# Two transformer blocks on one core: 128-row score products in block 2, and the order inside groups of small products

## The chip, the cores and the metric

The kernel runs on 1 core of a Trainium2 chip. The metric is device time in microseconds from launch to end, taken as the median of several runs. TensorE does the matrix products, VectorE and ScalarE the element-wise work, GpSimd a few powers and some transfers, and the DMA queues bring the weights. A profile of one execution goes with the times.

## The reference

The input is 256 rows of 1024 numbers. It passes through two layers of a first block (bidirectional mLSTM and dilated attention, a gated output, then a SwiGLU), and after them through two layers of a second block, which the change mostly concerns. A layer of the second block is

```
h = rms_norm(x); z, xbc, dt, q, k, v = split(h @ w_in)
xs, B, C = silu(conv7(xbc))                 # 16 heads of 64, 2 groups of 128 states
y_ssm  = ssd(xs, dt, B, C) forward + backward + d * xs;  y_ssm = rms_norm(y_ssm * silu(z))
s      = q k^T / 8 + bias(distance), |i-j| <= 128       # 16 heads of 64, 4 key heads
y_attn = softmax(s with a sink logit) @ v
x = x + [y_ssm, y_attn] @ w_out
h = rms_norm(x); x = x + (silu(conv3(h @ w_g)) * (h @ w_u)) @ w_down
```

Everything is in fp32. Activations and weights of the large products are split into a high part in fp32r (the rounded value) and a low part (the rest), and a product is three matmuls: high by high, low by high, high by low.

## The kernel before, in words

One core does all of it in one pass. Weights arrive in chunks of 1 MB in the order of `make_plan`; `emit_load` splits each half of a chunk, ScalarE making `hi` and VectorE `lo` (L473). `lin_st` (L520 to L522) multiplies a chunk with the normalized input and leaves pairs of 128 x 256 results in a PSUM bank (`lst`); `lin_units` (L612 to L614) does the output projections (`wo`, `ffo`). These are TensorE's bulk.

The order on each engine is made at build time. The framework lists instructions by priority and by when their inputs should be ready; `prio` raises or lowers the priority of a named kind of work, with the numbers of `PRIO1` and `PRIO2`. So small products are put between the large ones wherever the list finds them ready, and at run time each engine goes through its list in order, standing still where an input is missing.

A layer of block 2 runs in `mixer2` and `ffn2`. `mixer2` goes through the projections in the order of `PUMPS` and between them takes pieces of work from two lists:

- SSD, `ssd_quarter`: `mats` makes the decay matrices of a head (`sM`), `prod` (L1573) multiplies them with the inputs `xd` of two heads, one head in output partitions 0 to 63, one in 64 to 127, into the bank `sy`. A group is 8 products in plain fp32, each of which is two records in the trace.
- Attention, `attn`: `score(i)` makes the scores of one head for two blocks of 128 queries. The query tile `q2t` holds a head's 64 columns of q as fp32r in its own 64 partitions and the rest of the rounding in the other 64. The key tile `kst` holds the rounded key in both halves, so L1652 adds q_high k_high and q_low k_high in one product of 128 rows. L1653 adds q_high k_low from `kl`, which stands in the head's own 64 partitions only: a product with 64 rows. A group is L1652, L1653, L1652, L1653. `trans(i)` turns the probabilities (`qtr`, L1669: four transposes for two query blocks and two key blocks), `pv2_` (L1705) multiplies them with the values (`qo`: 8 products, two heads in the two halves of the output partitions), `rows_` spreads the softmax sums (`qrt`).

`keys` (L1777 to L1779) fills `kst` and `kl` once for each layer. Temporary tiles come from rings by size: `SHARED2` says how many buffers of each there are in block 2. The constants pool holds, among others, `cst` (identity, two triangles, and the mask of block 1's mLSTM in columns from `C_MK`) and the parameter vectors `pv1` of block 1; it lasts through the whole kernel. The temporary pool of block 1 is closed ahead of block 2's.

In block 1 the dilated attention's scores (`as`, L1221 and L1222) have 128 rows in both products, its values (`ao`, L1260) are 12 products with 64 output partitions, and the mLSTM's transposes are `mpt` (L1075).

Of the kernel before, what the change touches and what calls it, by code (L numbers as in the profile page):

```python
# [10 lines left out]
F32 = mybir.dt.float32  # L11
# [5 lines left out]
P = 128  # L17
T = 256
# [27 lines left out]
TR2 = (6, 4, 4)  # L46

SHARED1 = {512: 3, 1024: 5, 2048: 11, 4096: 5}
SHARED2 = {512: 3, 1024: 4, 2048: 11, 3072: 5, 4096: 2}

C_ID, C_TU, C_TL, C_MK = 0, 128, 256, 384
N_CST = 384 + 512

SEC = {"sh1": 0, "sc1": 1, "g1": 2, "sh2": 3, "sc2": 4, "g2": 5}

# [249 lines left out]
def two_blocks_kernel(ctx: ExitStack, tc: tile.TileContext, a: dict, out: bass.AP, stop=None):  # L305
# [5 lines left out]
    wp = ctx.enter_context(tc.tile_pool(name="weights", bufs=2))  # L311
    bp = ctx.enter_context(tc.tile_pool(name="big", bufs=8))
    pools = ExitStack()
    cur = {"tp": pools.enter_context(tc.tile_pool(name="tmp1", bufs=2)), "shared": SHARED1}
    lin = ctx.enter_context(tc.tile_pool(name="lin", bufs=4, space=bass.MemoryType.PSUM))
    sm = ctx.enter_context(tc.tile_pool(name="sm", bufs=4, space=bass.MemoryType.PSUM))
# [28 lines left out]
    ident = cst[:, C_ID:C_ID + P]  # L345
    triU = cst[:, C_TU:C_TU + P]
    triL = cst[:, C_TL:C_TL + P]
    mk = cst[:, C_MK:C_MK + 512]
    ones = cp.tile([P, P], F32, name="ones")
    V.memset(ones, 1.0)  # L350
    mhalf = cp.tile([P, 8], F32, name="mhalf")
# [8 lines left out]
    pv2 = []  # L360
    rw2 = []
    for l in range(DEPTH):
        pv1.append(cp.tile([P, a["pv1"].shape[2]], F32, name=f"pv1_{l}"))
        pv2.append(cp.tile([P, a["pv2"].shape[2]], F32, name=f"pv2_{l}"))
        rw2.append(cp.tile([P, 80], F32, name=f"rw2_{l}"))
    S.dma_start(pv1[0], a["pv1"][0])

    def late_params():
        S.dma_start(cst[:, P:], a["cst"][:, P:])
        S.dma_start(pv1[1], a["pv1"][1])  # L370
        for l in range(DEPTH):
            S.dma_start(pv2[l], a["pv2"][l])
            S.dma_start(rw2[l], a["rows2"][l:l + 1, :].to_broadcast([P, 80]))
# [575 lines left out]
    def mixer1(l, u, ob0=None, small=None, begun=None):  # L949
# [78 lines left out]
        def head(h, qT, kT, v):  # L1028
# [41 lines left out]

            def trans():
                tr = bank("mpt")
                for tt in range(2):
                    for c in range(2):
                        PE.transpose(tr[:, c * T + tt * P:c * T + (tt + 1) * P], s["p"][:, tt, c * P:(c + 1) * P],  # L1075
                                     ident)
                pt = tmp([2, T], "mPT")
                S.activation(pt, tr.rearrange("p (c t) -> p c t", c=2), AF.Copy)
                s["pt"] = pt
# [123 lines left out]
        def slots(j, qk):  # L1203


            s = {}
            sums = tmp([4], "asum")
            nm = tmp([4], "anm")
            r = tmp([4], "ar")

            def score(tt):
                def run():
                    tk = slice(tt * P, (tt + 1) * P)
                    sps = [bank("as") for _ in range(2)]
                    bs = []
                    for i in range(2):
                        bs.append(tmp([512], "abias"))
                        nc.sync.dma_start(bs[i], a["bt"][2 * j + i][:, tt, :])
                    for i in range(2):
                        q0, kh, kl = (qk[0][:, n, i, :] for n in range(3))  # L1220
                        PE.matmul(sps[i][:, :T], q0[:, tk], kh, start=True, stop=False)  # L1221
                        PE.matmul(sps[i][:, :T], q0[:, tk], kl, start=False, stop=True)  # L1222
                    for g in (1, 2):
                        for i in range(2):
                            o = sps[i][:, P + g * P:2 * P + g * P]
                            PE.matmul(o, qk[g][:, i, tk], qk["k"][:, g - 1, tk], start=True, stop=True)
                    for i in range(2):
                        e = 2 * tt + i
                        sp, b_ = sps[i], bs[i]
                        pt = tmp([512], "aP", bufs=4)  # L1230
                        V.tensor_tensor_reduce(pt, sp, b_, -1.0, -2 * NEG, ALU.add, ALU.min,
                                               nm[:, e:e + 1])
                        S.activation(pt, pt, AF.Exp, scale=-1.0, bias=nm[:, e:e + 1], accum_out=sums[:, e:e + 1])
                        s[i, tt] = pt
                return run

            def trans():
                V.reciprocal(r, sums)
                for i in range(2):
                    for b in range(2):  # L1240
                        tr = bank("apt")
                        for k in range(2):
                            for tt in range(2):
                                PE.transpose(tr[:, k * T + tt * P:k * T + (tt + 1) * P],
                                             s[i, tt][:, (2 * b + k) * P:(2 * b + k + 1) * P], ident)
                        pt = tmp([2, T], "aPT", bufs=4)
                        src = tr.rearrange("p (k t) -> p k t", k=2)
                        if b:
                            S.activation(pt, src, AF.Copy)
                        else:  # L1250
                            V.tensor_copy(pt, src)
                        s["t", i, b] = pt

            def pv_():
                o = bank("ao")
                for k, g, t0, n, vk in ((0, 0, 0, T, 0), (1, 0, 0, T, 1), (0, 1, 0, P, 0), (0, 1, P, P, 1),
                                        (1, 2, 0, P, 0), (1, 2, P, P, 1)):
                    for i in range(2):
                        c0 = (2 * j + i) * 64
                        PE.matmul(o[64 * i:64 * i + 64, t0:t0 + n], va[g][:, vk, c0:c0 + 64],  # L1260
                                  s["t", i, g > 0][:, k, t0:t0 + n], start=(k, g) == (0, 0), stop=(g, t0) == (2, P))
                for tt in range(2):
                    for i in range(2):
                        e = 2 * tt + i
                        PE.matmul(o[64 * i:64 * i + 64, T + tt * P:T + (tt + 1) * P],
                                  r[:, e:e + 1].to_broadcast([P, 64]), ident, start=True, stop=True)
                rb = tmp([T], "arb")
                S.activation(rb, o[:, T:], AF.Copy)
                os_ = tmp([T], "aos")
                V.tensor_tensor(os_, o[:, :T], rb, ALU.mult)  # L1270
                src = os_.rearrange("p (r i) -> p r i", r=2)
                dh = yb[0][:, j, :].rearrange("p (i r) -> p r i", r=2)
                dl = yb[1][:, j, :].rearrange("p (i r) -> p r i", r=2)
                S.activation(dh, src, AF.Copy)
                V.tensor_tensor(dl, src, dh.bitcast(F32), ALU.subtract)

            for n_, what, fn in zip(SLOT_AT, ("score", "score", "trans", "pv"), (score(0), score(1), trans, pv_)):
                defer(n_, with_prio("a_" + what, fn))
# [161 lines left out]
    def mixer2(l, u, zouts, small):  # L1440
# [95 lines left out]
        def ssd_quarter(i, xt):  # L1536
# [26 lines left out]
            def prod(pr):  # L1563
                def run():
# [3 lines left out]
                    xd = xds[i // 2][:, i % 2]  # L1568
                    o = s["y"][:, pr * T:(pr + 1) * T]
                    for d, c, m0, l0, n in ((0, 0, 0, 0, T), (1, 1, P, 0, T), (0, 1, T, P, P), (1, 0, 0, 0, P)):  # L1570
                        for k in range(2):
                            h = 2 * pr + k
                            PE.matmul(o[64 * k:64 * k + 64, l0:l0 + n], xd[:, d, c, 64 * h:64 * h + 64],  # L1573
                                      s[4 * i + h][:, d, m0:m0 + n], start=(d, c) == (0, 0), stop=(d, c) == (1, 0))
# [42 lines left out]
                made.update((c, c + 1))  # L1617

        kst = [tmp([2, T], f"kst{p}", F32R) for p in range(2)]
        kl = tmp([2, T], "kl", F32R)  # L1620
        vv = tmp([2, 256], "m_k")
        qts = {}

        def attn(c):
# [17 lines left out]
            def score(i):  # L1642
                def run():
                    hd = 4 * c + i
                    p = i % 2
                    own = slice(64 * p, 64 * p + 64)
                    kt = c // 2
                    sp = bank("qs")
                    pt = tmp([2, T], "qP", bufs=4)
                    for tt in range(2):  # L1650
                        q = qt[p][:, i // 2, tt * P:(tt + 1) * P]
                        PE.matmul(sp[:, tt * T:(tt + 1) * T], q, kst[p][:, kt, :], start=True, stop=False)  # L1652
                        PE.matmul(sp[:, tt * T:(tt + 1) * T], q[own], kl[own, kt, :], start=False, stop=True)  # L1653
                    for tt in range(2):
                        e = 2 * i + tt
                        w0 = 128 - 128 * tt
# [7 lines left out]
            def trans(i):  # L1664
                def run():
                    tr = bank("qtr")
                    for tt in range(2):
                        for k in range(2):
                            PE.transpose(tr[:, k * T + tt * P:k * T + (tt + 1) * P], s[i][:, tt, k * P:(k + 1) * P],  # L1669
                                         ident)  # L1670
# [28 lines left out]
            def pv2_():  # L1699
                o = bank("qo")  # L1700
                for pr in range(2):
                    for k in range(2):
                        for i in range(2):
                            kv = 2 * (c // 2) + i
                            PE.matmul(o[64 * i:64 * i + 64, pr * T:(pr + 1) * T], vv[:, k, kv * 64:(kv + 1) * 64],  # L1705
                                      s["t", 2 * pr + i][:, k, :], start=k == 0, stop=k == 1)
# [65 lines left out]
        def keys():  # L1772
            ps = st("k2")
            for p in range(2):
# [1 line left out]
                src = ps[own].rearrange("p (c t) -> p c t", c=2)  # L1776
                S.activation(kst[p][own], src, AF.Copy)  # L1777
                S.activation(kst[p][other], src, AF.Copy)
                V.tensor_tensor(kl[own], src, kst[p][own].bitcast(F32), ALU.subtract)  # L1779

        def values():
            w = chunk("v2", l)
# [135 lines left out]
```

## Time and profile before

| | |
|---|---|
| median of 3 runs | 1934.13 us (1933.36 to 1936.22) |
| profiled execution | 1935.3 us, span 1933.5 us, mean granted clock 0.997 |
| TensorE (PE) | 1890.2 us busy, 13022 matmuls |
| VectorE (DVE) | 1465.9 us busy |
| ScalarE (ACT) | 1085.0 us busy |
| DMA | 388.09 MB, mean 201 GB/s |

A row of the timeline gives the start in us from the span's first instruction, the duration, engine, line, operation, the tiles written and read, the form (rows times columns of the array, then the moving operand) and how many records are merged in it. Matmuls overlap in the array: a duration holds the passage through it, so the pace is read from the distance between two starts. PEld is the load of a product's stationary operand.

### The profile page before, as it was taken

Reading aid. Unit: us, or ns where it says so; the run is one execution under the profiler, and the core shown is the slowest. Engines: PE = TensorE matmul, PEld = TensorE weight load, DVE = VectorE, ACT = ScalarE, POOL = GpSimd, SP = SyncE. Lnnn points to the kernel's source line nnn. Section 1 sums busy time; section 2 is a strip of 40 time slices with the busy share of each in tenths; the row PEclk is TensorE's granted clock in tenths of the full one; section 3 lists DMA queues with packets and bytes.
Section 4 is the critical chain, followed back from the end, with each engine's and each line's share of the span. In section 5 each row is a group of like instructions: output and inputs, shape, how many; then the busy total and the mean of one; then the engine's idle time right before and its main releaser. Section 6 shows DMA issues by size and latency. Waiting matters only on the chain.

```text
span 1933.5 us, 32684 instructions
## 1 busy us (share of the span) xinstructions
PE 1890.2 (98%) x13022; PEld 1710.4 (88%) x13022; DVE 1465.9 (76%) x2555; ACT 1085.0 (56%) x1881; POOL 87.5 (5%) x108
## 2 busy tenths in 40 slices
PE   6999999999999999999999999999999999999998
PEld 5889999899978899999899888778998898779996
DVE  8888877787767787868766578877876688768763
ACT  3556654454436566544544457876554577756552
POOL 0000000200010000000200001000000000000000
PEclk9999999999999999999999999999999999999999
DMA  8654777487745446767377636444555454345552
GB/s 313 253 185 161 265 248 275 154 292 287 272 153 196 175 169 222 249 255 261 137 272 281 230 111 181 132 128 174 196 192 183 171 184 152 107 169 188 192 179 86
DMA packets 64202, 388.09 MB, mean 201 GB/s; under 512 B 7611, under 2 KB 12395, under 8 KB 21554
## 3 DMA queue, kind: packets, MB, share of 16 engines
q1 hardware_dynamic: 58064, 364.93, 52.3%
q0 software_dynamic: 4832, 20.13, 3.5%
q8 instruction: 102, 1.67, 0.3%
q10 hardware_dynamic: 1154, 0.95, 0.2%
q14 instruction: 50, 0.41, 0.1%
HBM read 384.82 MB, written 5.36 MB: 202 GB/s over the span
## 4 chain that ended last, share of the span: by engine, by line
PE 88%; DVE 5%; ACT 3%; DMA 1%; issue 1%; POOL 0%; POOLq 0%; DVEq 0%; ACTq 0%
PE lst L520 17%; PE lst L521 17%; PE lst L522 17%; PE ffo L613 4%; PE ffo L612 4%; PE ffo L614 4%; PE wo L612 2%; PE wo L613 2%; PE wo L614 2%; PE sy L1573 2%; PE qs L1653 1%; PE qo L1705 1%; PE avl L553 1%; PE avl L554 1%; PE avl L555 1%
## 5 line engine op out<-in xcount | busy, mean ns | idle before, releaser
L473 ACT ACTIVATE hi<-raw 128x1024 fp32r<-128x1024 f32 x546 | 571.7, 1057 | 499.0 <-PE lst L521 302.0
L473 DVE TENSOR_TENSOR lo<-raw,hi 128x1024 fp32r<-128x1024 f32 x546 | 662.5, 1221 | 229.5 <-ACT hi L473 228.7
L520 PE MATMUL lst<-uh,hi 128*128 128x256 f32 x2592 | 743.9, 287 | 0.0
L522 PE MATMUL lst<-uh,lo 128*128 128x256 f32 x2592 | 737.8, 285 | 0.2
L521 PE MATMUL lst<-ul,hi 128*128 128x256 f32 x2592 | 737.9, 285 | 0.0
L520 PEld LDWEIGHTS lst<-uh,hi 128*128 128x128 f32 x2592 | 496.6, 192 | 5.1 <-issue 3.9
L522 PEld LDWEIGHTS lst<-uh,lo 128*128 128x128 f32 x2592 | 496.7, 192 | 4.5 <-issue 3.5
L521 PEld LDWEIGHTS lst<-ul,hi 128*128 128x128 f32 x2592 | 496.8, 192 | 3.3 <-issue 2.1
L412 DVE CUSTOM_DVE_ANT_0 raw<-raw,crow,pv 128x1024 f32<-128x1024 f32 x96 | 120.9, 1280 | 27.6 <-DMA raw<-in_ws_dram 27.5
L612 PE MATMUL ffo<-hi,ffh 128*128 128x512 f32 x352 | 137.3, 390 | 0.0
L613 PE MATMUL ffo<-lo,ffh 128*128 128x512 f32 x352 | 137.0, 389 | 0.0
L614 PE MATMUL ffo<-hi,ffl 128*128 128x512 f32 x352 | 137.0, 389 | 0.0
L942 DVE SCALAR_TENSOR_TENSOR cacc<-cin,pv,cacc 128x254 f32<-128x254 f32 (+2 forms) x272 | 111.6, 478 | 0.3 <-ACT cacc L935 0.2
L614 PEld LDWEIGHTS ffo<-hi,ffl 128*128 128x128 f32 x352 | 66.1, 188 | 13.7
L612 PEld LDWEIGHTS ffo<-hi,ffh 128*128 128x128 f32 x352 | 66.1, 188 | 13.5
L613 PEld LDWEIGHTS ffo<-lo,ffh 128*128 128x128 f32 x352 | 66.1, 188 | 13.5
L774 DVE TENSOR_TENSOR ul<-uf,uh 128x256 fp32r<-128x256 f32 (+1 forms) x35 | 26.4, 755 | 26.7 <-ACT uh L769 26.7
L1555 ACT ACTIVATE sM<-arow,ac 128x128 f32<-128x128 f32 x128 | 44.9, 389 | 0.0
L1402 ACT ACTIVATE rsq<-xres 128x512 f32<-128x512 f32 x20 | 12.5, 627 | 53.3 <-DVE xres L1865 21.6
L553 PE MATMUL mvh<-hi,uh 128*128 128x512 f32 x80 | 33.4, 418 | 8.1 <-ACT uh L865 8.1
L555 PE MATMUL ltt<-hib,ul 128*128 128x512 f32 x72 | 29.7, 413 | 7.7 <-DVE ul L774 5.5
L766 ACT ACTIVATE uf<-tr,ub,us 128x128 f32<-128x128 f32 x36 | 14.3, 451 | 39.9 <-PE tr L752 39.9
(381 smaller groups left out, 3004.4 us busy)
## 6 DMA issues: line engine op xcount, KB each, us to landing
raw<-in_ws_dram SPq DMA_DIRECT2D x329, 1024.0 KB, 4.9
abias<-in_bt_dram SPq DMA_DIRECT2D x32, 256.0 KB, 4.7
arow<-scra POOLq DMA_DIRECT2D x32, 256.0 KB, 5.4
wtab<-skew SPq DMA_DIRECT2D x16, 384.0 KB, 3.6
gb<-in_rows_dram POOLq DMA_DIRECT2D x8, 512.0 KB, 5.8
skew<-scrt POOLq DMA_DIRECT2D x4, 1024.0 KB, 11.9
raw<-in_ws_dram SPq DMA_DIRECT2D x6, 512.0 KB, 8.9
grow<-scrg POOLq DMA_DIRECT2D x2, 1024.0 KB, 6.3
```

The source lines that it names most:

```text
L412: V.tensor_tensor_reduce(src, src, crow, 1.0, pv1[l][:, 136 + sec * 8 + ct:137 + sec * 8 + ct], ALU.mult, ALU.add, ada[l, sec][:, ct:ct + 1])
L473: fn()
L520: PE.matmul(outp, sh, mh, start=first, stop=False)
L521: PE.matmul(outp, sh, ml, start=False, stop=False)
L522: PE.matmul(outp, sl, mh, start=False, stop=last)
L553: PE.matmul(outs[tt], sl[0], hi[:, i, :], start=kt == first, stop=False)
L555: PE.matmul(outs[tt], sl[1], hi[:, i, :], start=False, stop=kt == last)
L612: PE.matmul(o, sh, hi[:, i, :], start=kt == first, stop=False)
L613: PE.matmul(o, sh, lo[:, i, :], start=False, stop=False)
L614: PE.matmul(o, sl, hi[:, i, :], start=False, stop=kt == last)
L942: V.scalar_tensor_tensor(acc[:, c, lo:hi], src[:, lo + s:hi + s], cw[:, k0 + j:k0 + j + 1], acc[:, c, lo:hi], ALU.mult, ALU.add)
L1555: S.activation(m[:, d, 2 * tt * P:(2 * tt + 1) * P], rt[:, d, hh, tt * P:(tt + 1) * P], AF.Relu, scale=-1.0, bias=ac[:, tt, col])
```

## The change

- `keys` makes `klt`, one tile for each parity of head, with the low part of the keys in both halves of the partitions; L1653 multiplies the whole query tile with it, 128 rows. That adds q_low k_low, which was left out before.
- One more buffer of 2 KB in block 2. The mask `mk` and `pv1` move to a pool of their own, which is closed with the temporaries of block 1; `mk` gets a transfer of its own.
- In five groups of small products the loops run so that the first product reads the input that is made last.

```diff
-SHARED2 = {512: 3, 1024: 4, 2048: 11, 3072: 5, 4096: 2}
+SHARED2 = {512: 3, 1024: 4, 2048: 12, 3072: 5, 4096: 2}
-N_CST = 384 + 512
+N_CST = 384
...
+    cp1 = pools.enter_context(tc.tile_pool(name="const1", bufs=1))
...
-    mk = cst[:, C_MK:C_MK + 512]
+    mk = cp1.tile([P, 512], F32, name="mk")
...
-        pv1.append(cp.tile([P, a["pv1"].shape[2]], F32, name=f"pv1_{l}"))
+        pv1.append(cp1.tile([P, a["pv1"].shape[2]], F32, name=f"pv1_{l}"))
...
-        S.dma_start(cst[:, P:], a["cst"][:, P:])
+        S.dma_start(cst[:, P:], a["cst"][:, P:N_CST])
+        S.dma_start(mk, a["cst"][:, C_MK:C_MK + 512])
...   block 1: head.trans (mpt)
-                for tt in range(2):
+                for tt in (1, 0):
...   block 1: slots.pv_ (ao)
-                for k, g, t0, n, vk in ((0, 0, 0, T, 0), (1, 0, 0, T, 1), (0, 1, 0, P, 0), (0, 1, P, P, 1),
-                                        (1, 2, 0, P, 0), (1, 2, P, P, 1)):
-                    for i in range(2):
+                for k, g, t0, n, vk in ((0, 1, 0, P, 0), (0, 1, P, P, 1), (1, 2, 0, P, 0), (1, 2, P, P, 1),
+                                        (0, 0, 0, T, 0), (1, 0, 0, T, 1)):
+                    for i in (1, 0):
...   block 2: ssd_quarter.prod (sy)
-                        for k in range(2):
+                        for k in (1, 0):
...   block 2: mixer2
-        kl = tmp([2, T], "kl", F32R)
+        klt = [tmp([2, T], f"klt{p}", F32R) for p in range(2)]
...   block 2: attn.score (qs)
-                        PE.matmul(sp[:, tt * T:(tt + 1) * T], q[own], kl[own, kt, :], start=False, stop=True)
+                        PE.matmul(sp[:, tt * T:(tt + 1) * T], q, klt[p][:, kt, :], start=False, stop=True)
...   block 2: attn.trans (qtr)
-                    for tt in range(2):
+                    for tt in (1, 0):
...   block 2: attn.pv2_ (qo)
-                        for i in range(2):
+                        for i in (1, 0):
...   block 2: keys
-                V.tensor_tensor(kl[own], src, kst[p][own].bitcast(F32), ALU.subtract)
+                for h in (own, other):
+                    V.tensor_tensor(klt[p][h], src, kst[p][own].bitcast(F32), ALU.subtract)
```

The start and stop marks of the `ao` group move with its order.

## Rows read from the trace of the kernel before

**Rows 1.** The page: busy us, share of the span and instructions of each engine.
```profile
PE 1890.2 (98%) x13022; PEld 1710.4 (88%) x13022; DVE 1465.9 (76%) x2555; ACT 1085.0 (56%) x1881; POOL 87.5 (5%) x108
```

**Rows 2.** Windows: stretch, its length, busy us of each engine, clock, DMA.
```profile
1180.00:1300.00 120.00, 118.47 (x816) 93.13 (x816) 97.38 (x206) 98.21 (x242) 7.09 (x13) 1.00 0.44 133
...
1580.00:1700.00 120.00, 120.00 (x812) 92.84 (x812) 93.99 (x197) 93.84 (x231) 6.42 (x11) 1.00 0.41 131
...
1240.00:1260.00 20.00, 20.00 (x152) 16.45 (x151) 18.26 (x32) 17.50 (x42) 2.13 (x4) 1.00 0.68 220
```

**Rows 3.** Timeline of TensorE's matmuls around one score group: start, duration.
```profile
1255.42 0.28 PE L521 MATMUL lst<-ul,hi 128*128 128x256 f32 x1
1255.54 0.28 PE L1652 MATMUL qs<-kst,q2t 128*128 128x256 f32 x1
1255.74 0.38 PE L1653 MATMUL qs<-kl,q2t 64*128 64x256 f32 x1
1256.06 0.39 PE L1652 MATMUL qs<-kst,q2t 128*128 128x256 f32 x1
1256.37 0.38 PE L1653 MATMUL qs<-kl,q2t 64*128 64x256 f32 x1
1256.68 0.39 PE L522 MATMUL lst<-uh,lo 128*128 128x256 f32 x1
1256.90 0.28 PE L520 MATMUL lst<-uh,hi 128*128 128x256 f32 x1
```

**Rows 4.** Instructions on the tile kl: duration ns min/median/max, first and last start.
```profile
L1653 PE MATMUL qs<-kl,q2t x64: 378/381/384, 1188.0 to 1682.9; 64*128 64x256 f32 x64
L1779 DVE TENSOR_TENSOR kl<-lst,kst x4: 676/688/695, 1181.5 to 1575.9; 64x512 fp32r<-64x512 f32 x4
```

**Rows 5.** Instructions of line L1222, block 1's second score product.
```profile
L1222 PE MATMUL as<-aqs x32: 278/283/283, 195.4 to 826.0; 128*128 128x256 f32 x32
```

**Rows 6.** Timeline of TensorE's weight loads in the same score group.
```profile
1256.37 0.18 PEld L1653 LDWEIGHTS qs<-kl,q2t 64*128 64x128 f32 x1
...
1256.79 0.19 PEld L520 LDWEIGHTS lst<-uh,hi 128*128 128x128 f32 x1
```

**Rows 7.** Timeline of TensorE: sy, qo and ao groups, torn and whole.
```profile
1698.08 0.40 PE L614 MATMUL wo<-hi,mixal 128*128 128x512 f32 x1
1698.31 0.39 PE L612 MATMUL wo<-hi,mixah 128*128 128x512 f32 x1
1698.63 0.65 PE L1573 MATMUL sy<-sM,xd 128*64 128x256 f32 x2
1699.21 0.50 PE L613 MATMUL wo<-lo,mixah 128*128 128x512 f32 x1
1699.55 0.40 PE L614 MATMUL wo<-hi,mixal 128*128 128x512 f32 x1
1699.87 1.51 PE L1573 MATMUL sy<-sM,xd 128*64 128x256 f32 x14
...
1295.29 1.52 PE L1573 MATMUL sy<-sM,xd 128*64 128x256 f32 x16
...
1192.11 0.65 PE L1573 MATMUL sy<-sM,xd 128*64 128x256 f32 x2
...
1241.52 0.65 PE L1705 MATMUL qo<-qPT,m_k 128*64 128x256 f32 x2
...
1686.90 0.65 PE L1705 MATMUL qo<-qPT,m_k 128*64 128x256 f32 x2
...
845.64 1.96 PE L1260 MATMUL ao<-aPT,av 128*64 128x256 f32 x24
```

**Rows 8.** Waits from 1141 to 1737, TensorE: us in total, times, longest.
```profile
PE sy L1573 <- DVE xd L1528: 1.1, 1, 1.1
```

**Rows 9.** Instructions on the tile qP, ScalarE.
```profile
L1659 ACT ACTIVATE qP<-qP,qnm x64: 491/497/511, 1194.3 to 1685.8; 128x256 f32<-128x256 f32 x64
L1659 ACT ACTIVATION_READ_ACCUMULATOR qP<-qP,qnm x64: 185/188/193, 1194.8 to 1686.2; 128x1 f32 x64
```

More of the change, by code (lines that the diff above doesn't have):

```diff
@@ L1255, in pv_ @@
                 o = bank("ao")
-                for k, g, t0, n, vk in ((0, 0, 0, T, 0), (1, 0, 0, T, 1), (0, 1, 0, P, 0), (0, 1, P, P, 1),
-                                        (1, 2, 0, P, 0), (1, 2, P, P, 1)):
-                    for i in range(2):
+                for k, g, t0, n, vk in ((0, 1, 0, P, 0), (0, 1, P, P, 1), (1, 2, 0, P, 0), (1, 2, P, P, 1),
+                                        (0, 0, 0, T, 0), (1, 0, 0, T, 1)):
+                    for i in (1, 0):
                         c0 = (2 * j + i) * 64
                         PE.matmul(o[64 * i:64 * i + 64, t0:t0 + n], va[g][:, vk, c0:c0 + 64],
-                                  s["t", i, g > 0][:, k, t0:t0 + n], start=(k, g) == (0, 0), stop=(g, t0) == (2, P))
+                                  s["t", i, g > 0][:, k, t0:t0 + n], start=(g, t0) == (1, 0), stop=(k, g) == (1, 0))
                 for tt in range(2):
@@ L1645, in run @@
                     p = i % 2
-                    own = slice(64 * p, 64 * p + 64)
                     kt = c // 2
```

## The prediction

> **What bounds the kernel now.** I read the page first. Its row of busy times shows TensorE in a matmul for 98% of the span, VectorE for 76%, ScalarE for 56% [rows 1]: the end is set by TensorE's own stream, and an edit pays if it shortens that stream where nobody else is as full. Next I cut block 2's two mixers out with the windows view, since nearly all of the change lies there: in the 120 us from 1180 TensorE is busy for 118.5 us, VectorE for 97.4 and ScalarE for 98.2; in the 120 us from 1580 it is 120.0, 94.0 and 93.8, all at the full granted clock (1.00) [rows 2]. TensorE waits there for almost nothing: the largest row for one of the lines that are edited is 1.1 us [rows 8].
>
> Busy is not the same as dense, so I went to the timeline of TensorE and read starts, not durations. Between two `lst` products of 256 columns a start follows the other after 0.12 us (1255.42 to 1255.54). In a score group they follow after 0.20, 0.32, 0.31 and 0.31 us (1255.54, 1255.74, 1256.06, 1256.37, 1256.68), and the first `lst` behind it needs 0.22 (1256.68 to 1256.90) [rows 3]. All these products stream 256 columns. What differs is the form: L1652 is 128\*128, L1653 is 64\*128, and each change of form costs about 0.2 us.
>
> **Part 1: the second score product with 128 rows.** The group of four and the `lst` behind it take 1.36 us from 1255.54 to 1256.90 [rows 3]. If no form changes, five products at 0.12 take 0.60. Saved: 0.76 us. L1653 stands 64 times in the trace, two to a group, so there are 32 groups in the two layers [rows 4]: 32 x 0.76 = 24.3 us. That 128 rows on both sides bring the short interval is seen in block 1, whose score products L1221 and L1222 are built that way: the 32 of L1222 take 0.28 us each as the `lst` do, where L1653 takes 0.38 [rows 5]. Bounds: a group whose successor is a 64-column run keeps that one change, which leaves some 0.2 us less (0.56); if all were so, 17.9 us. Where all five intervals were the 0.31 of the inner ones the group would give 0.95, 30 us in all.
>
> One rule of the Trainium skill speaks against this part. "TensorE: Matmul & The Clock Gate", section "Step-by-step: what each phase is for", says that the engine pulls a weight load ahead of matmuls in flight when the row groups don't conflict or the load goes to the background buffer, and that the number of rows plays no part in a load's time. By that rule a load of 64 rows would hide like any other and the form would cost nothing. The loads show otherwise: the one of L520 starts at 1256.79, 0.11 us before its matmul at 1256.90, but the one of L1653 starts at 1256.37 together with its matmul [rows 3, 6]. What the rule would make of the time is the rival "no effect" below.
>
> **Part 2: what the 128 rows cost.** `klt` takes two VectorE subtractions for each half where `kl` took one: four more of 0.69 us in the kernel, 2.8 us [rows 4]. They lie beside `lst` products of a busy TensorE; uncovered they would cost those 2.8 us. The score products wait for both; they stand some 6 us after the keys (1181.5 to 1188.0 for the first) [rows 4], so 0.7 us each can be late without being met. The ring of 2 KB tiles gets its twelfth buffer for the one long-lived tile that is added, so as many rotate as before. The room is that of `mk` and `pv1`, whose readers are all in block 1; `mk` has its own copy on ScalarE's queue in place of a part of the one for `cst`, the same bytes in one more issue. I take zero for these, with 1 us as an upper bound.
>
> **Part 3: groups that begin with the input made last.** In block 2 the 64-column groups are often torn: a first product starts alone as soon as its own input is there, then other work runs, and the rest comes later. A product in plain fp32 is two records, so a lone start reads "x2". Price from one in full: the form changes (1698.31 to 1698.63 is 0.32 us, where `wo` products follow after 0.23), the lone start lasts 0.58 (1698.63 to 1699.21), and the `wo` behind it needs 0.34 instead of 0.23: 0.09 + 0.58 + 0.11 = 0.78 us [rows 7]. Nothing of that comes back in the rest: its 14 records last 1.51 us, a whole group's 16 last 1.52, because the partner in the other 64 columns runs beside it [rows 7]. Lone starts: ten of `sy` (L1573), from 1192.11 to 1698.63, and four of `qo` (L1705), from 1241.52 to 1686.90 [rows 7]. With k or i running (1, 0), the group's head needs the later input, so the group should come whole: 14 x 0.78 = 10.9 us. Lower bound zero (the list tears them at other places); upper bound, since three more groups are torn in the middle, about 14.
>
> The transposes (`qtr`, `mpt`) are 128\*128 like the `lst`; whether two and two or four together, no form changes: I take zero. In block 1 all eight `ao` groups already run as 24 records in one piece [rows 7], and so do the `mpt` groups: zero, or at worst one lone start for each of the eight `ao`, 6 us, if the new order tears them.
>
> **What comes late next.** TensorE's stream loses 24.3 + 10.9 = 35.2 us, half in each mixer, 17.6. In the first, 120 us would become 102.4, with 97.4 + 1.4 us of VectorE work and 98.2 of ScalarE in them, 96% each. The densest 20 us in which both are loaded, those from 1240, show 18.26 us of VectorE, 91%, beside 17.5 of ScalarE [rows 2]. At 91% the first mixer needs 98.8 / 0.91 = 108.6 us, which gives back 6.2; the second (94.0 + 1.4) / 0.91 = 104.8 against 102.4, which gives back 2.4. Together 8.6 us. Ends of this term: 0 if VectorE can run at 97%, and the whole gain if it can't do better than the 81% of now.
>
> **Sum.** -35.2 + 8.6 = -26.6 us. The profiled execution took 1935.3 us (span 1933.5 and 1.8 around it), 1.2 above the median of the runs, 1934.1. I take the difference to the median: 1934.1 - 26.6 = 1907.5 us.
>
> **Rivals.**
> (a) Nothing is given back: VectorE and ScalarE hide all of it. 1934.1 - 35.2 = 1899 us. For it: VectorE's waits there are mostly for TensorE, and shrink with it. Against: 96% on two engines at once is seen nowhere in these mixers [rows 2].
> (b) Part 1 pays, part 3 doesn't, because the order is by list and the groups break elsewhere. -24.3 + 3 (12.2 us off each mixer leaves about 0.8 and nothing over 91%; I allow 3) = 1913 us. For it: three groups are torn for other reasons than the first input.
> (c) The followers bind: VectorE and ScalarE stay near 85%. Then the first mixer needs 98.8 / 0.85 = 116 us and the second 112, a gain of only 4 + 8 = 12 us: 1922. Between this and the forecast all values can occur.
> (d) No effect: the slow interval comes from something else that the two products share (the same weights loaded twice, the chained accumulation), by the rule above. 1934 us. Against: block 1's pairs have the same chain and run at full pace [rows 5].
> (e) Slower. TensorE runs in order. A group whose head waits for the later input stands in front of all `lst` products behind it, where before its first half filled that time. 32 `qtr` groups whose second input comes 0.50 + 0.19 us after the first [rows 9], and 24 groups of `sy` and `qo`, where lone start and rest lay at least 1.2 us apart (1698.63, 1699.87 [rows 7]): 22 + 29 = 51 us, 24 more than the 26.6 won: 1958 us. It decides from a mean wait of 26.6 / 56 = 0.48 us at each head. For it: lone starts exist because inputs come apart. Against: the order puts other products ahead of a group that isn't ready, and TensorE's waits on these lines are 1.1 us now [rows 8].
>
> **How the numbers follow.** Forecast 0.50, with its own range 1901 to 1914; (a) 0.14; (b) 0.14; (c) 0.12; (d) 0.04; (e) 0.06. The range 1896 to 1923 takes in (a), (b) and most of (c), and leaves out some 0.15. No change means within 0.2% (3.9 us), about what a measurement of this kernel can tell. Faster: 0.90; same: 0.04; slower: 0.06.
>
> **What would show it.** Part 1: no 64\*128 form is left, and score products follow each other after 0.12 us. Part 2: eight subtractions on L1779's successor instead of four. Part 3: no `sy` or `qo` run of "x2" alone. Late next: VectorE above 88% in the mixers, with TensorE's waits there still at a few us. I am wrong if the interval of the score products stays at 0.3, if the lone starts come back on other lines, or if TensorE's waits on L1573, L1669 or L1705 grow past 10 us.

## The result and the profile after

The changed kernel takes 1908.5 us (median of 4 runs, 1907.8 to 1909.3) against 1933.7 before: ratio 0.987, 95% interval 0.985 to 0.989. Measured again beside other kernels it gave 1908.7, ratio 0.986 (0.985 to 0.988). The forecast was 1907.5.

The page's row of busy times, which answers to [rows 1]:

```profile
PE 1859.1 (98%) x13022; PEld 1699.3 (89%) x13022; DVE 1467.7 (77%) x2559; ACT 1084.7 (57%) x1881; POOL 88.1 (5%) x108
```

TensorE does as many matmuls in 31 us less busy time. VectorE has four more instructions and 1.8 us more.

TensorE's timeline around a score group (against [rows 3]; the lines of the kernel have moved by one or two):

```profile
1232.57 0.28 PE L1653 MATMUL qs<-kst,q2t 128*128 128x256 f32 x1
1232.69 0.28 PE L1654 MATMUL qs<-klt,q2t 128*128 128x256 f32 x1
1232.81 0.28 PE L1653 MATMUL qs<-kst,q2t 128*128 128x256 f32 x1
1232.93 0.28 PE L1654 MATMUL qs<-klt,q2t 128*128 128x256 f32 x1
1233.05 0.28 PE L522 MATMUL lst<-uh,hi 128*128 128x256 f32 x1
1233.17 0.28 PE L523 MATMUL lst<-ul,hi 128*128 128x256 f32 x1
```

Every start now follows the last after 0.12 us: 0.60 from 1232.57 to 1233.17, where the same five took 1.36. The weight load of the second product starts 0.12 us ahead of it (1232.57 for the matmul at 1232.69), where the one of the old L1653 began together with its matmul [rows 3, 6]:

```profile
1232.57 0.19 PEld L1654 LDWEIGHTS qs<-klt,q2t 128*128 128x128 f32 x1
```

The instructions on `klt` (against [rows 4]):

```profile
L1654 PE MATMUL qs<-klt,q2t x64: 276/282/287, 1189.6 to 1661.3; 128*128 128x256 f32 x64
L1781 DVE TENSOR_TENSOR klt<-lst,kst x8: 676/688/697, 1180.7 to 1566.5; 64x512 fp32r<-64x512 f32 x8
```

The timeline where `sy` had begun with a lone pair (against [rows 7]). The transposes come four together, the `sy` group whole with its 16 records:

```profile
1195.71 0.60 PE L1670 MATMUL qtr<-cst,qP 128*128 128x128 f32 x4
1196.48 1.52 PE L1575 MATMUL sy<-sM,xd 128*64 128x256 f32 x16
```

Nowhere is a `sy` or `qo` group begun by a lone product any more. Not every group comes whole, though: two `sy` groups (from 1210.7 and from 1595.9) are still torn in the middle by transposes, and single `sy` products stand there.

The two mixers of block 2 in the windows view, each from its first small product to the start of the next normalization: the two stretches of the kernel before, then of the changed one (length; busy us of PE, PEld, DVE, ACT, POOL; clock; DMA).

```profile
1141.00:1332.90 191.90, 189.12 (x1292) 157.52 (x1290) 157.96 (x321) 137.71 (x310) 11.06 (x20) 1.00 0.50 163
1534.10:1736.90 202.80, 200.96 (x1344) 165.74 (x1342) 162.04 (x319) 142.32 (x314) 12.35 (x20) 0.99 0.48 160
```
```profile
1139.90:1322.50 182.60, 177.25 (x1292) 153.95 (x1291) 158.68 (x323) 136.73 (x311) 12.00 (x20) 0.98 0.51 171
1523.70:1709.30 185.60, 183.17 (x1344) 158.79 (x1342) 162.75 (x321) 140.97 (x314) 11.99 (x20) 1.00 0.52 175
```

The lengths say where the time came from: 9.3 us in the first mixer, 17.2 in the second, 26.5 of the 27.6 us by which the span is shorter. TensorE's busy time in both fell from 390.1 to 360.4, by 29.7 us; its idle time (length less busy time) rose from 4.6 to 7.8. The waits of TensorE in the changed kernel from 1139.9 to 1709.3 (us in total, times, longest):

```profile
PE xst L1521 <- DVE xbc L948: 1.9, 1, 1.9
PE grs L1611 <- POOL grt L383: 1.5, 2, 0.8
PE wo L614 <- ACT mixah L1714: 1.5, 1, 1.5
PE wo L614 <- ACT mixsh L1617: 0.9, 2, 0.4
PE gss L1602 <- DVE gsq L1599: 0.7, 2, 0.4
```

The first was there before. The other four, 4.6 us, are at the ends of the mixers, where `wo` needs the last attention output and the last group norm; before, only one `grs` wait of 1.4 us stood there.

### The profile page after: what moved, and what is told of

It is laid out like the page before. It is cut to its first block, busy times and chain, and to the rows that moved or that the text cites. A ratio compares the mean times of both kernels' runs of the same rounds, so it can differ in the third digit from the quotient of the medians.

```text
span 1905.9 us, 32680 instructions
## 1 busy us (share of the span) xinstructions
PE 1859.1 (98%) x13022; PEld 1699.3 (89%) x13022; DVE 1467.7 (77%) x2559; ACT 1084.7 (57%) x1881; POOL 88.1 (5%) x108
## 4 chain that ended last, share of the span: by engine, by line
PE 88%; ACT 5%; DVE 4%; issue 1%; DMA 1%; POOL 0%; POOLq 0%; ACTq 0%
PE lst L522 17%; PE lst L523 17%; PE lst L524 17%; PE ffo L615 4%; PE ffo L614 4%; PE ffo L616 4%; PE wo L614 2%; PE wo L616 2%; PE wo L615 2%; PE sy L1575 1%; ACT hi L475 1%; PE avl L555 1%; PE avl L556 1%; PE avl L557 1%; PE mvh L555 1%
## 5 line engine op out<-in xcount | busy, mean ns | idle before, releaser
L557 PE MATMUL ltt<-hib,ul 128*128 128x512 f32 x72 | 29.7, 412 | 7.7 <-DVE ul L776 5.5
```

What stands on the lines that cost most here:

```text
L557: PE.matmul(outs[tt], sl[1], hi[:, i, :], start=False, stop=kt == last)
```

## The experiments

Each comparison is a median with the ratio to the kernel before, measured on the same chip in turn (1934.6 to 1935.0 us there), with its 95% interval. "Runs" are unbroken stretches of 64-column products in TensorE's built order (67 before, 50 in the changed kernel).

**128 rows alone.** In the changed kernel all five loop orders are as before, here that of `sy`:

```diff
-                        for k in (1, 0):
+                        for k in range(2):
```

> Part 1 alone: klt, 128 rows in the second score product, the room for it, all five loop orders as before. Change-of-form theory: score products 0.12 us apart, 24.3 us less TensorE stream, of which a few us come back: 1911 to 1914 us. The lone starts of sy and qo (17 in the order as built, against 16 before) stay. Rival 'no effect of the form': 0.3 us apart as before, 1934 us. Rival 'the order of the groups is the larger part': above 1920 us.

1910.9 us, ratio 0.988 (0.986 to 0.989). Windows of its mixers:

```profile
1141.00:1321.60 180.60, 177.41 (x1292) 153.46 (x1290) 158.68 (x323) 137.35 (x310) 11.45 (x20) 1.00 0.52 173
1522.80:1712.40 189.60, 188.84 (x1343) 161.06 (x1342) 162.48 (x322) 141.86 (x314) 11.43 (x20) 1.00 0.52 171
```

TensorE's busy time is 366.24 instead of 390.09, 23.9 less, and its idle time 4.0 instead of 4.6 (its waits there: `xst` 1.6, `sy` 1.2 and 0.6, `qtr` 0.3): part 1, with the room that it needs, is worth what it was priced at, nothing of it came back, and it is nearly the whole change.

**The order alone**, on the kernel before, with 64 rows: the five loop edits of the change and nothing else of it, here that of `qo`.

```diff
-                        for i in range(2):
+                        for i in (1, 0):
```

> Part 3 alone: the five loop orders, with kl and 64 rows as before. Torn-group theory: lone starts of sy and qo go from 16 to 4 in the order as built, 12 to 14 times 0.78 us: 1923 to 1925 us. Rival (b), the order pays nothing: 1934 us. Rival (e), group heads stand and wait: TensorE's waits on L1573, L1669 and L1705 grow and the time is above 1938 us.

1928.6 us, ratio 0.997 (0.996 to 0.998): 6 us, little more than half of the 10 to 12 that were expected. Its windows:

```profile
1139.40:1332.00 192.60, 185.44 (x1292) 155.16 (x1290) 157.87 (x321) 137.48 (x310) 11.96 (x20) 1.00 0.50 162
1533.30:1729.80 196.50, 194.36 (x1343) 164.25 (x1341) 161.56 (x319) 141.74 (x314) 12.34 (x20) 0.99 0.49 165
```

TensorE's busy time falls by 10.3 us (390.1 to 379.8), close to the 10.9 of the torn groups. But its idle time rises from 4.6 to 9.3 us. Rival (e) is there, in small: a `qo` group's head stands 1.6 us for its transposed input, `grs` for 2.2 at the mixers' ends:

```profile
PE grs L1609 <- POOL grt L381: 2.2, 2, 1.4
PE qo L1705 <- ACT qPT L1673: 1.6, 1, 1.6
```

**The room alone**: the pool, the twelfth buffer and `mk`'s transfer, with `kl`, 64 rows and the old orders.

```diff
-SHARED2 = {512: 3, 1024: 4, 2048: 11, 3072: 5, 4096: 2}
+SHARED2 = {512: 3, 1024: 4, 2048: 12, 3072: 5, 4096: 2}
...
-    mk = cst[:, C_MK:C_MK + 512]
+    mk = cp1.tile([P, 512], F32, name="mk")
```

> Only the room: mk and pv1 in a pool that is closed with block 1, 12 buffers of 2 KB, mk's own transfer; kl, 64 rows and loop orders as before. My theory: nothing of it costs or gains by itself, 1934 us, within 1 us. Rival: more buffers let the list arrange the work otherwise; the order as built has 75 runs of 64-column products where before has 67, at 0.34 to 0.78 us each 3 to 6 us slower: 1937 to 1940 us.

1937.8 us, ratio 1.0013 (1.0004 to 1.0022). The rival was right in direction: the room costs some 2.5 us (0.8 to 4.3 by the interval). TensorE's busy time in the mixers is 2.6 us longer (392.7), with 75 runs, so the other order of the list is the likely cause; nothing else was tried.

**64 rows, grouped**, on the kernel before:

```diff
-                        PE.matmul(sp[:, tt * T:(tt + 1) * T], q, kst[p][:, kt, :], start=True, stop=False)
+                        PE.matmul(sp[:, tt * T:(tt + 1) * T], q, kst[p][:, kt, :], start=tt == 0, stop=False)
+                    for tt in range(2):
+                        q = qt[p][:, i // 2, tt * P:(tt + 1) * P]
-                        PE.matmul(sp[:, tt * T:(tt + 1) * T], q[own], kl[own, kt, :], start=False, stop=True)
+                        PE.matmul(sp[:, tt * T:(tt + 1) * T], q[own], kl[own, kt, :], start=False, stop=tt == 1)
```

> The kernel before with one thing changed: a score group is issued L1652, L1652, L1653, L1653 (64 rows kept, half as many changes of form). Change-of-form theory: group and the lst behind it take 0.12 + 0.20 + 0.12 + 0.31 + 0.22 = 0.97 us instead of 1.36, 32 groups give 12.5 us: about 1922 us. Rival 'a product with 64 rows is slow by itself': the two of them stay 0.31 us apart and the time is 1930 to 1934 us.

1923.0 us, ratio 0.994 (0.992 to 0.995), as the theory had it. A group in its timeline, between `lst` products, and the second 64-row product of that group, which a narrower window shows by itself:

```profile
1646.41 0.40 PE L1652 MATMUL qs<-kst,q2t 128*128 128x256 f32 x2
1646.74 0.50 PE L1655 MATMUL qs<-kl,q2t 64*128 64x256 f32 x2
1647.17 0.38 PE L522 MATMUL lst<-uh,lo 128*128 128x256 f32 x1
1647.39 0.28 PE L520 MATMUL lst<-uh,hi 128*128 128x256 f32 x1
```
```profile
1646.96 0.28 PE L1655 MATMUL qs<-kl,q2t 64*128 64x256 f32 x1
```

From 1646.41 to 1647.39 these are 0.98 us, and my sum was 0.97, but its terms were not right: two 64-row products in a row stand 0.22 us apart (1646.74, 1646.96), where I had put 0.12, and the way out takes 0.21 (1646.96 to 1647.17) instead of 0.31. The first `lst` behind the change, with 128 rows, needs the same 0.22 (1647.17 to 1647.39). So a change of form costs about 0.09 us in the interval ahead of it and 0.10 in the one behind it, 0.2 in all, and a single 64-row product between 128-row ones has both in one interval (0.31). What costs is the change of form; a cost of the 64 rows themselves is not seen. No run has three of them in a row, so their own pace isn't shown.

**The changed kernel again**, without an edit, as a yardstick.

> The changed kernel once more, beside the others of this call, so that differences of 2 to 5 us can be read: 1908.5 us, ratio 0.987.

1908.7 us, ratio 0.986 (0.985 to 0.988).

**More work for VectorE**, in the changed kernel:

```diff
-                V.scalar_tensor_tensor(qt[other], src, 0.125, qt[own].bitcast(F32), ALU.mult, ALU.subtract)
+                for _ in range(3):
+                    V.scalar_tensor_tensor(qt[other], src, 0.125, qt[own].bitcast(F32), ALU.mult, ALU.subtract)
```

> The changed kernel with 16 more VectorE operations of 0.69 us in each mixer of block 2 (the low parts of the query tiles are written three times instead of once), 11 us a mixer; VectorE would be busy for 169 of the first mixer's 181 us instead of 158. My forecast's term (VectorE and ScalarE give back above 91%): (169 / 0.91 = 186) 5 us more in the first mixer and some in the second, 1914 to 1918 us. Rival 'what comes back is waits of TensorE at group heads, and VectorE's share has no part in it': not above 1910 us; the order as built has 40 runs of 64-column products instead of 50, at 0.34 us each 3 us less: 1905.

1925.9 us, ratio 0.995 (0.994 to 0.997): 17 us slower than the changed kernel, more than either theory gave. Windows, and the longest waits of TensorE:

```profile
1138.90:1331.60 192.70, 176.87 (x1292) 152.69 (x1291) 170.69 (x339) 137.97 (x311) 11.99 (x20) 0.99 0.48 162
1532.80:1730.30 197.50, 186.73 (x1344) 162.54 (x1343) 174.91 (x338) 142.58 (x314) 11.97 (x20) 0.97 0.48 164
```
```profile
PE qtr L1670 <- ACT qP L1660: 5.7, 7, 3.0
PE qs L1653 <- DVE q2t L1741: 4.6, 3, 2.2
```

VectorE is busy for 89% in both windows (170.7 of 192.7, 174.9 of 197.5), but that is a mean over stages. In the dense stretch of the first mixer it is 96%, and TensorE falls to 89% there:

```profile
1185.00:1288.00 103.00, 91.36 (x719) 77.00 (x719) 99.13 (x206) 83.94 (x215) 5.32 (x10) 1.00 0.43 139
```

TensorE idles 26.6 us in the two mixers. So VectorE's work can hold them back, but with 12 us more than the change gives it. The added operations also stand straight ahead of the score products, which wait 4.6 us for `q2t`; whether the full VectorE or this longer chain costs more was not separated.

**Less work for VectorE**, in the kernel with the `qrt` priority (next): two of the seven taps of block 2's convolution are left out, which the result needs.

```diff
-                    if j == m:
+                    if j == m or (ntap == 7 and j in (0, 6)):
```

> The kernel with the higher priority for qrt (1900.3 us, 41 runs of 64-column products) with two of the seven taps of block 2's convolution left out: 24 VectorE operations of 0.48 us, 11.5 us less VectorE work in each mixer; 42 runs. If VectorE's share (89 to 90% in that kernel's mixers) holds TensorE back: 1890 to 1895 us. If TensorE's own stream is the bound and VectorE only just keeps up: 1898 to 1902 us.

1899.9 us, ratio 0.982 (0.981 to 0.984), the same as the 1900.3 without that edit. Its windows, then that kernel's:

```profile
1139.10:1317.70 178.60, 174.48 (x1292) 154.06 (x1291) 149.82 (x299) 136.51 (x311) 12.36 (x20) 0.99 0.51 175
1519.00:1701.40 182.40, 179.89 (x1342) 158.00 (x1341) 154.40 (x297) 140.99 (x314) 11.43 (x20) 1.00 0.52 178
```
```profile
1140.60:1320.30 179.70, 174.45 (x1292) 153.08 (x1291) 158.57 (x323) 136.94 (x311) 11.44 (x20) 0.99 0.52 174
1521.50:1701.80 180.30, 179.32 (x1343) 158.01 (x1342) 162.34 (x322) 140.95 (x314) 11.43 (x20) 1.00 0.53 180
```

VectorE has 8.8 and 7.9 us less to do, and the two mixers together are no shorter (361.0 us against 360.0). VectorE doesn't hold that kernel back, at 88 and 90% of its mixers.

**A higher priority for `qrt`**, in the changed kernel, whose timeline had six single `qrt` pairs between single `lst` products:

```diff
-            return out + [with_prio("pv", fn) for fn in (pv2_, rows_, fin)]
+            return out + [with_prio("pv", pv2_), with_prio("score", rows_), with_prio("pv", fin)]
```

> The changed kernel with a higher priority for the step that spreads the softmax sums (qrt), so that its groups aren't parted by single lst products: 41 runs of 64-column products in the order as built instead of 50. If each run costs two changes of form whatever it holds: 9 x 0.34 = 3 us less, 1905 us. Rival 'the list only moves the waits': 1908 us or more, with longer waits of TensorE.

1900.3 us, ratio 0.982 (0.980 to 0.983): 8.4 us faster than the changed kernel, for nine runs fewer, nearly three times the 3 us that I expected. The single `qrt` pairs are gone from its timeline; in the mixers TensorE is busy for 353.8 us instead of 360.4 and idle for 6.2 instead of 7.8. How much of that the pairs make up was not tried by itself.

**Without the turned transposes**: the changed kernel with `sy` and `qo` turned; `mpt`, `qtr` and `ao` as before, here `qtr`.

```diff
-                    for tt in (1, 0):
+                    for tt in range(2):
```

> The changed kernel with the transposes (mpt, qtr) and ao in the order before; sy and qo keep the new order. Transposes are 128*128 like lst, so their order saves no change of form. If their heads bring part of the waits that came back: 1905 to 1907 us, with less idle time of TensorE than the changed kernel. If not: 1908.5 us, the order as built has 51 runs of 64-column products against 50.

1903.8 us, ratio 0.984 (0.982 to 0.985), 4.9 us faster than the changed kernel, though it has one run more. Windows:

```profile
1139.00:1317.50 178.50, 174.21 (x1291) 151.59 (x1290) 158.71 (x323) 137.47 (x311) 11.44 (x20) 1.00 0.52 175
1518.80:1702.70 183.90, 180.86 (x1342) 157.53 (x1341) 162.36 (x321) 141.15 (x314) 11.43 (x20) 1.00 0.54 176
```

Against 128 rows alone TensorE's busy time is 11.2 us less (366.24 to 355.07), its idle time 3.3 more (4.0 to 7.3). Against the changed kernel its idle time is only 0.5 us less (7.8 to 7.3) and its busy time 5.3 (360.4 to 355.1), so waits are the smaller part of the 4.9 us. Some 2.7 us of the rest are the lower clock, at which the changed kernel's profile runs for 6.8 us of the first mixer (0.98 in its window, 1.00 here), priced as in the last section.

**Only the transposes `qtr` turned**, with 128 rows; against 128 rows alone:

```diff
-                    for tt in range(2):
+                    for tt in (1, 0):
```

> 128 rows, and of the five loop orders only that of the transposes qtr; sy, qo, mpt and ao as before. The order as built has 63 runs of 64-column products against 68 with 128 rows alone (1910.9 us). Theory 'the turned transposes bring waits and no change of form': 1911 to 1915 us with more waits of TensorE on L1670 or at the end of the mixers. Rival 'they cost nothing, and the 5 us between the changed kernel and the one without them are chance of the list': 1907 to 1910 us, fewer runs and no more waits.

1917.3 us, ratio 0.992 (0.990 to 0.993): 6.4 us slower than 128 rows alone, in spite of five runs fewer. The waits that 128 rows alone doesn't have, the windows, and one stretch of the first:

```profile
PE wo L614 <- ACT mixah L1714: 1.6, 1, 1.6
PE grs L1611 <- POOL grt L383: 1.5, 2, 0.8
PE wo L614 <- ACT mixsh L1617: 0.9, 2, 0.4
PE gss L1602 <- DVE gsq L1599: 0.8, 2, 0.4
```
```profile
1142.20:1328.60 186.40, 180.04 (x1291) 154.73 (x1290) 158.77 (x323) 136.80 (x311) 12.01 (x20) 0.98 0.50 167
1529.90:1721.40 191.50, 189.24 (x1343) 162.46 (x1342) 163.01 (x321) 141.48 (x314) 11.99 (x20) 0.99 0.51 170
1290.60:1297.30 6.70, 6.70 (x30) 4.29 (x32) 4.04 (x5) 1.68 (x2) 1.63 (x1) 0.50 0.51 174
```

They are the changed kernel's own end-of-mixer waits, 1.5, 1.5, 0.9 and 0.7 there. TensorE idles 4.6 us more in the mixers than with 128 rows alone (8.6 against 4.0) and is busy 3.0 us longer. Some 10 us of that busy time, the 6.7 shown and 3.4 from 1696.7, run at the lower clock, which the mixers of 128 rows alone never do; at the pace of the last section this is some 4 us.

**`qrt` priority with the old order of the transposes** and `ao`: the kernel without the turned transposes, and

```diff
-            return out + [with_prio("pv", fn) for fn in (pv2_, rows_, fin)]
+            return out + [with_prio("pv", pv2_), with_prio("score", rows_), with_prio("pv", fin)]
```

> The higher priority of the qrt step together with the old order of the transposes and ao: 49 runs of 64-column products in the order as built, 8 more than with the new order of the transposes (1900.3 us). If runs decide: 8 x 0.34 to 8 x 0.78 more, 1903 to 1906 us. If the waits behind the turned transposes decide: 1896 to 1900 us.

1900.6 us, ratio 0.983 (0.981 to 0.984). The same as with the new order, with eight runs more: TensorE is busy for 354.1 us in the mixers against 353.8, and idle for 5.7 against 6.2. With this priority neither the runs nor the turned transposes decide. The 0.34 us for a run that several expectations use is not borne out: nine runs fewer came with 8.4 us less, eight more with nothing, and five fewer with 6.4 us more.

**`qrt` priority and 128 rows, all old orders**: 128 rows alone, with the same edit of the priority.

> 128 rows, all five loop orders as before, and the higher priority of the qrt step: 57 runs of 64-column products in the order as built against 68 with 128 rows alone (1910.9 us), with 20 lone starts of sy and qo left. If each run costs 0.34 us of changes and a lone one more: 11 runs fewer give 4 to 8 us, 1903 to 1907 us. If the list only moves the waits: 1910 us or more.

1907.2 us, ratio 0.986 (0.985 to 0.988), 3.7 less than without the priority. The intervals of the two overlap, so this is likely and not shown.

## Why the prediction was right, and where it wasn't

**Part 1** was right in mechanism and size: 24.3 us forecast; 23.7 measured alone, 23.9 in TensorE's busy time. The rival "no effect" fell with 128 rows alone: there the two products still share an accumulation and load the same weights twice, and follow each other after 0.12 us. That a product with 64 rows is slow by itself is what the grouped run speaks against.

**Part 3, `sy` and `qo`,** was right in what it saves and wrong in what that is worth. The torn groups were priced at 10.9 us; TensorE's busy time fell by 10.3 (order alone) and 11.2 (on top of 128 rows). But only 7.1 us reached the end (1910.9 to 1903.8): some 3 went into idle time of TensorE. In the changed kernel even that is nearly gone: it lies 2 us below 128 rows alone, within the intervals of both.

**Part 3, the transposes,** was taken as zero, and that step failed. Turned on their own they cost 6.4 us; the changed kernel is 4.9 us slower than the one with transposes and `ao` in the old order. No form changes, as I said; but I left out that four transposes begun only when the second input is there end later, and that at a mixer's end `qPT`, `qo`, `mixah` and `wo` hang on the last of them. The wait of `wo` for `mixah` fits that: 1.6 and 1.5 us in the two kernels, and none in the two with the old order of the transposes. The rest of the 6.4 us is less clear. The waits on `grs`, `gss` and `mixsh` belong to the group norm of SSD, which no transpose feeds, and some 4 us are the lower clock. Nor is the price fixed: with the `qrt` priority both orders take 1900 us. So the zero was wrong for this list, and the cause beyond the 1.6 us stays open. I put the price of waiting heads into rival (e) alone and all or nothing, where a part of it belonged into the sum.

**What comes late next**: this step named the wrong cause. I took 8.6 us back because VectorE and ScalarE would not pass 91% in the stretches that I had cut out. In the changed kernel the like stretches, 103 us long, have VectorE at 92% and ScalarE at 90%, then at 90 and 88%, with TensorE busy for 99.6 and 99.3%:

```profile
1180.00:1283.00 103.00, 102.58 (x798) 87.77 (x796) 95.22 (x202) 93.07 (x235) 6.24 (x12) 0.99 0.48 154
1566.00:1669.00 103.00, 102.24 (x800) 86.81 (x799) 92.79 (x196) 91.06 (x233) 6.40 (x12) 1.00 0.53 164
```

So next to nothing is given back there (0.4 and 0.8 us of idle time). Less work for VectorE brought nothing either, and 128 rows alone gave nothing back. The total of 1907.5 came so close by luck: the two real losses, some 3 us of idle time with `sy` and `qo` and 4.9 with the transposes, come to 8 us, the size of the term that had no ground. The share was not a vain question: with 12 us more work VectorE stands at 96% of such a stretch, and TensorE waits.

**Part 2** was right: `klt` shows as eight subtractions of 0.69 us and costs nothing seen. Room alone is some 2.5 us slower, above the 1 us that I allowed, probably through the list's order.

The two kernels that add the `qrt` priority to turned `sy` and `qo` beat all of these, at 1900 us.

## What to carry to other kernels

When one engine's stream is the bound, read the distance between starts: products of equal size at 0.12 and 0.31 us differed in the form here, and fewer changes of form paid in full, whole groups in part (7.1 of 11.2 us). Turn a group to its last-made input where that saves a change of form; where it saved none, the turn bought nothing and cost between nothing and 6.4 us, as the list lay around it. Read an engine's share in the stage that you argue about: a mean over the whole mixer hid a VectorE at 96%. When two parts are tried together, try each alone: here the better part carried the other's loss.

## What was not expected

TensorE's granted clock can fall right after it has waited. In the changed kernel `gss`, `grs` and `wo` wait 0.4, 0.8 and 0.4 us between 1294.8 and 1298.1, and from 1299.1 on 3.4 us run at 0.50, the lower of the two levels, 1.2 GHz:

```profile
1299.10:1302.50 3.40, 3.40 (x10) 2.63 (x9) 3.40 (x7) 1.84 (x3) 0.00 (x0) 0.50 0.00 0
1302.50:1306.00 3.50, 3.50 (x17) 2.88 (x16) 1.77 (x3) 2.07 (x3) 0.00 (x0) 1.00 0.76 269
```
```profile
1298.86 0.39 PE L615 MATMUL wo<-lo,mixsh 128*128 128x512 f32 x1
1299.09 0.59 PE L616 MATMUL wo<-hi,mixsl 128*128 128x512 f32 x1
1299.47 0.63 PE L614 MATMUL wo<-hi,mixsh 128*128 128x512 f32 x1
```

There `wo` products follow after 0.38 us (1299.09 to 1299.47) instead of 0.23 (1298.86 to 1299.09), so 3.4 us of it cost 3.4 x (1 - 0.23 / 0.38) = 1.3 us more, on top of the wait. Windows with a clock of 0.98 or 0.99 hold such stretches: the changed kernel and the one with only `qtr` turned have them, as has the second mixer before; 128 rows alone and the one without turned transposes don't (1.00 in both windows).

A wait is not always followed by a fall. The changed kernel was profiled twice. In the first profile `xst` waits 1.9 us up to 1179.6 and the clock falls; in the second it waits 1.6 us up to 1178.7 and the clock stays. The stretch behind the wait, in the first and in the second:

```profile
1179.70:1183.10 3.40, 3.40 (x13) 3.04 (x14) 3.32 (x6) 3.34 (x10) 1.07 (x2) 0.51 0.36 105
```
```profile
1178.70:1182.10 3.40, 3.40 (x26) 3.30 (x27) 3.32 (x6) 3.36 (x9) 1.06 (x2) 1.00 0.54 130
```

With the `qrt` priority and the old transposes `xst` waits 2.0 us and the clock stays as well. What decides is not shown here, and part of a difference of one or two us between two profiles can be this clock.
